# Gelu-and-multiply on one core: the second half of the first tile loaded through ScalarE's DMA queue instead of SyncE's

## The chip, the cores and the metric

The kernel runs on one core of one Trainium2 chip. The metric is the device time of one execution in microseconds (us); of several runs the median counts. Before the change three runs took 469.28, 469.09 and 472.29 us, median 469.28 us.

## What is computed

The input x has 32 x 512 rows of 2048 float32 numbers, 134.2 MB; the output has 1024 numbers for each row, 67.1 MB. The first half of each row goes through gelu and is multiplied by the second half:

```python
def reference(x: np.ndarray) -> np.ndarray:
    half_dim = x.shape[-1] // 2
    x1, x2 = (x[..., :half_dim].copy(), x[..., half_dim:].copy())
    gelu_x1 = 0.5 * x1 * (1 + erf(x1 / np.sqrt(2)))
    return (gelu_x1 * x2).astype(np.float32)
```

## The kernel before

The 16384 rows are cut into 16 tiles. A tile has 128 partitions with R = 8 consecutive rows in each, so a load of a whole tile brings 64 KB into each partition (8.39 MB), and a store of a whole tile takes 32 KB out of each (4.19 MB). There are two input buffers and two output buffers; tile i uses buffer i % 2 of each.

ScalarE computes the gelu from the input buffer into the output buffer (line 81), and VectorE multiplies the output buffer by the second half of the input in place (line 89). A middle tile is done in two pieces, of 5 and 3 rows; tile 0 and the last tile, 15, in three, of 2, 2 and 4 rows.

All waits are written by hand. Loads are issued by SyncE (`load`, line 46). Stores are issued by ScalarE's queue, in line with its gelus (`store`, line 51), except for those of tiles 14 and 15, which SyncE issues. A store first waits until VectorE has multiplied all that it takes out (semaphore mul_done). Tile 0 and tile 15 are stored in two halves of 4 rows; here they are called 0a, 0b, 15a and 15b.

Three loads stand ahead of the loop, in the program's first block (lines 60 to 64): the first half of tile 0 (rows 0 to 3 of each partition), its second half (rows 4 to 7), and all of tile 1. Each half of tile 0 has a semaphore of its own, first[0] and first[1]; ScalarE waits for it before the gelu of rows 0 to 1 and of rows 4 to 7 (lines 76 and 77). The block is closed at lines 66 and 67, where all engines meet. After that, load i + 2 is issued by SyncE as soon as tile i has been multiplied (lines 108 and 109). Load i + 2 and the store of tile i count on the same semaphore, ready[i % 2]; the first gelu of tile i + 2 waits for both (line 79), since it needs its input and overwrites the output buffer that the store reads.

ScalarE works in order. The store of 0a, with its wait for VectorE, stands on it ahead of the gelu of rows 4 to 7.

Of the kernel before, what the change touches and what calls it, by code (L numbers as in the profile page):

```python
# [1 line left out]

# [4 lines left out]

GELU = mybir.ActivationFunctionType.Gelu


@with_exitstack
def kernel(
    ctx: ExitStack,
    tc: tile.TileContext,
    x: bass.AP,
    out: bass.AP,
):
    nc = tc.nc
    P = nc.NUM_PARTITIONS

    x_flat = x.flatten_outer_dims()
    out_flat = out.flatten_outer_dims()
    n_rows, dim = x_flat.shape
    half = dim // 2

    R = 8
    x_t = x_flat.rearrange("(n p r) d -> n p r d", p=P, r=R)
    o_t = out_flat.rearrange("(n p r) d -> n p r d", p=P, r=R)
    n_tiles = x_t.shape[0]
    x_bufs = [nc.alloc_sbuf_tensor(f"x{k}_tile", [P, R, dim], x.dtype) for k in range(2)]  # L30
    o_bufs = [nc.alloc_sbuf_tensor(f"o{k}_tile", [P, R, half], out.dtype) for k in range(2)]

    first = [nc.alloc_semaphore(f"first{j}") for j in range(2)]
    ready = [nc.alloc_semaphore(f"ready{k}") for k in range(2)]
    gelu_done = nc.alloc_semaphore("gelu_done")
    mul_done = nc.alloc_semaphore("mul_done")
    tail_stored = nc.alloc_semaphore("tail_stored")
    n = {sem.name: 0 for sem in [*first, *ready, gelu_done, mul_done, tail_stored]}  # L40

    def counted(ins, sem, by):
        ins.then_inc(sem, by)
        n[sem.name] += by

    def load(i, rows, sem):
        ins = nc.sync.dma_start(out=x_bufs[i % 2][:, rows, :], in_=x_t[i][:, rows, :])  # L47
        counted(ins, sem, 16)
        return ins

    def store(queue, i, rows, sem):
        queue.wait_ge(mul_done, n[mul_done.name])
        counted(
            queue.dma_start(out=o_t[i][:, rows, :], in_=o_bufs[i % 2][:, rows, :]), sem, 16
        )

    for ins in (  # L60
        load(0, slice(0, 4), first[0]),
        load(0, slice(4, 8), first[1]),
        load(1, slice(0, 8), ready[1]),
    ):
        tc.no_tile_sem_insts.add(ins.ins.name)
    tc.close()
    tc.compile()  # L67

    for i in range(n_tiles):
        k = i % 2  # L70
        last = i == n_tiles - 1
        pieces = i == 0 or last
        steps = ((0, 2), (2, 4), (4, 8)) if pieces else ((0, 5), (5, 8))
        for lo, hi in steps:
            rows = slice(lo, hi)
            if i == 0 and lo % 4 == 0:
                nc.scalar.wait_ge(first[lo // 4], 16)
            elif lo == 0:
                nc.scalar.wait_ge(ready[k], n[ready[k].name])
            counted(  # L80
                nc.scalar.activation(  # L81
                    out=o_bufs[k][:, rows, :], in_=x_bufs[k][:, rows, :half], func=GELU
                ),
                gelu_done,
                1,
            )
            nc.vector.wait_ge(gelu_done, n[gelu_done.name])
            counted(
                nc.vector.tensor_mul(  # L89
                    out=o_bufs[k][:, rows, :],  # L90
                    in0=o_bufs[k][:, rows, :],
                    in1=x_bufs[k][:, rows, half:],
                ),
                mul_done,
                1,
            )
            if pieces and hi % 4 == 0:
                if last:
                    store(nc.sync, i, slice(hi - 4, hi), tail_stored)
                else:  # L100
                    store(nc.scalar, i, slice(hi - 4, hi), ready[k])
        if not pieces:
            if i == n_tiles - 2:
                store(nc.sync, i, slice(0, R), tail_stored)
            else:
                store(nc.scalar, i, slice(0, R), ready[k])
        if i + 2 < n_tiles:
            nc.sync.wait_ge(mul_done, n[mul_done.name])
            load(i + 2, slice(0, R), ready[k])


    nc.scalar.drain()  # L112
    for sem in (*first, *ready):
        nc.scalar.sem_clear(sem)
    nc.vector.drain()
    nc.vector.sem_clear(gelu_done)
    nc.sync.sem_clear(mul_done)
    nc.sync.wait_ge(tail_stored, n[tail_stored.name]).then_inc(
        tail_stored, -n[tail_stored.name]
    )  # L120


# [1 line left out]
_INS = ['x']  # L124
_OUTS = [((32, 512, 1024), 'float32')]


# [23 lines left out]
```

## Time and profile before

| What | Value |
|---|---|
| median of three runs | 469.28 us (469.09 to 472.29) |
| span of the profiled execution, first to last instruction | 467.9 us |
| median of the runs less that span | 1.4 us |
| DMA, whole span | 201.34 MB, 430 GB/s |
| VectorE busy | 140.5 us |
| ScalarE busy | 115.5 us |
| first half of tile 0: issue to landing | 12.0 us, from 0.73 |
| second half of tile 0: issue to landing | 21.3 us, from 1.16 |
| load 1: issue to landing | 45.5 us, from 1.64 |
| store 0a: issue to landing | 28.1 us, from 19.23 |
| store 0b: issue to landing | 41.0 us, from 30.57 |
| a middle load, a middle store: issue to landing | 44.2 us, 44.7 us |

The profile gives the span of the profiled execution and no other time of it; what lies around the span is read from the difference to the median. Times within the profile count from its first instruction. In the queue rows, q1 is the queue through which SyncE issues and q10 the one through which ScalarE issues; the columns are packets, MB, and the time that the packets took as a share of 16 DMA engines. In the row of tenths, each digit is one of 40 equal slices of the span. In a group's row there stand the count, the busy time, the mean duration in ns, and the idle time ahead of the group with what ended it. "SPq" and "ACTq" rows are issues of DMAs.

### The profile page before, as it was taken

The page shows a single profiled execution, that of the slowest core. Times are in us where ns is not written, and L with a number is a line of the kernel's source. Part 1 is how long each engine was busy: PE and PEld are TensorE (multiplying, and loading weights), DVE is VectorE, ACT ScalarE, POOL GpSimd, SP SyncE. Part 2 cuts the span into 40 slices and gives each one's busy share as a digit, 9 for nine tenths or more (in the row PEclk, how much of TensorE's full clock was granted, in tenths as well). Part 3 has the DMA queues.
Part 4 walks back from the last instruction along what each step waited for, and adds up shares of the span by engine and source line. Part 5 has one row for each costly group of instructions (what it writes and reads, how often), then busy time and mean ns, then how long its engine had stood idle before and what let it go on. Part 6 is the DMA issues. An engine that isn't in the chain of part 4 may idle for free.

```text
span 467.9 us, 152 instructions
## 1 busy us (share of the span) xinstructions
DVE 140.5 (30%) x34; ACT 115.5 (25%) x35; POOL 0.2 (0%) x4
## 2 busy tenths in 40 slices
DVE  0330514207052060511606116060150702507043
ACT  1320606042060410604106050050500506014060
POOL 0000000000000000000000000000000000000000
DMA  8999999999999999999999999999999999999998
GB/s 359 448 448 443 403 405 492 409 403 448 459 437 403 434 417 493 403 403 448 476 420 403 445 406 493 403 406 445 487 409 403 445 451 448 403 434 417 493 389 373
DMA packets 5041, 201.34 MB, mean 430 GB/s; under 512 B 560, under 2 KB 560, under 8 KB 560
## 3 DMA queue, kind: packets, MB, share of 16 engines
q1 hardware_dynamic: 2880, 142.61, 70.6%
q10 hardware_dynamic: 2160, 58.72, 29.1%
q14 instruction: 1, 0.01, 0.0%
HBM read 134.22 MB, written 67.11 MB: 430 GB/s over the span
## 4 chain that ended last, share of the span: by engine, by line
DMA 76%; DVE 14%; ACT 8%; ACTq 0%; SPq 0%; issue 0%
DMA out_dram<-o_tile 66%; DVE o_tile L89 14%; DMA x_tile<-in_x_dram 10%; ACT o_tile L81 8%; ACTq L112 0%; SPq L47 0%
## 5 line engine op out<-in xcount | busy, mean ns | idle before, releaser
L89 DVE TENSOR_TENSOR o_tile<-o_tile,x_tile 128x5120 f32<-128x5120 f32 (+3 forms) x34 | 140.5, 4171 | 319.7 <-ACT o_tile L81 319.7
L81 ACT ACTIVATE o_tile<-x_tile 128x5120 f32<-128x5120 f32 (+3 forms) x34 | 114.3, 3407 | 337.4 <-DMA out_dram<-o_tile 301.6
L81 ACT ACT_TABLE_LOAD x1 | 1.3, 1283 | 2.9 <-PEq L67 2.9
L135 POOL MEMSET const-bfloat16-1.0<- 128x1 bf16 x1 | 0.1, 101 | 0.0
L135 POOL MEMSET const-uint8-127<- 128x1 uint8 x1 | 0.1, 101 | 0.0
L135 POOL MEMSET const-float32-0.0<- 128x1 f32 x1 | 0.1, 98 | 0.2 <-issue 0.2
L135 POOL MEMSET const-float32-1.0<- 128x1 f32 x1 | 0.1, 98 | 0.0
## 6 DMA issues: line engine op xcount, KB each, us to landing
out_dram<-o_tile ACTq DMA_DIRECT2D x13, 4096.0 KB, 44.7
x_tile<-in_x_dram SPq DMA_DIRECT2D x2, 4096.0 KB, 16.6
out_dram<-o_tile ACTq DMA_DIRECT2D x2, 2048.0 KB, 34.5
out_dram<-o_tile SPq DMA_DIRECT2D x1, 4096.0 KB, 25.2
out_dram<-o_tile SPq DMA_DIRECT2D x2, 2048.0 KB, 7.8
x_tile<-in_x_dram SPq DMA_DIRECT2D x15, 44.2
```

The source lines that it names most:

```text
L81: nc.scalar.activation(out=o_bufs[k][:, rows, :], in_=x_bufs[k][:, rows, :half], func=GELU),
L89: nc.vector.tensor_mul(out=o_bufs[k][:, rows, :], in0=o_bufs[k][:, rows, :], in1=x_bufs[k][:, rows, half:],),
L135: nc = _bacc.Bacc("TRN2", target_bir_lowering=False, num_devices=1)
```

## The change

`load` gets a parameter for the engine that issues, with SyncE as its default, and the load of the second half of tile 0 is issued by ScalarE. Its place in the program, its semaphore and the data that it moves stay.

```diff
-    def load(i, rows, sem):
-        ins = nc.sync.dma_start(out=x_bufs[i % 2][:, rows, :], in_=x_t[i][:, rows, :])
+    def load(i, rows, sem, queue=nc.sync):
+        ins = queue.dma_start(out=x_bufs[i % 2][:, rows, :], in_=x_t[i][:, rows, :])
         counted(ins, sem, 16)
         return ins
...
     for ins in (
         load(0, slice(0, 4), first[0]),
-        load(0, slice(4, 8), first[1]),
+        load(0, slice(4, 8), first[1], nc.scalar),
         load(1, slice(0, 8), ready[1]),
     ):
```

## The prediction

> **What bounds the kernel now.** I read the page first, for the busy shares and the DMA row; then the chain of waits in order of time, for what releases each tile; then the DMA view of single stretches, for how the two queues share the engines; then the timeline of the first 48 us and of the end. The page:
>
> ```profile
> DVE 140.5 (30%) x34; ACT 115.5 (25%) x35; POOL 0.2 (0%) x4
> DMA  8999999999999999999999999999999999999998
> DMA packets 5041, 201.34 MB, mean 430 GB/s; under 512 B 560, under 2 KB 560, under 8 KB 560
> L81 ACT ACTIVATE o_tile<-x_tile 128x5120 f32<-128x5120 f32 (+3 forms) x34 | 114.3, 3407 | 337.4 <-DMA out_dram<-o_tile 301.6
> ```
>
> Both compute engines idle two thirds of the span; the DMA engines are at 90% or more in every slice but the first and the last. 201.34 MB at the 434 GB/s of the steady stretch below is 464 us of the 467.9 us span. So the time is DMA work plus whatever leaves the engines empty, and an edit that moves transfers without emptying them can only shift work about. The chain, two pieces of the loop and the end:
>
> ```profile
> 1.64 45.54 DMA x_tile<-in_x_dram
> 47.20 4.48 ACT o_tile L81
> 51.70 8.77 DVE o_tile L89 x2
> 60.50 40.04 DMA out_dram<-o_tile
> 100.56 4.48 ACT o_tile L81
> ...
> 403.86 44.69 DMA out_dram<-o_tile
> 448.56 1.91 ACT o_tile L81
> ```
>
> A tile waits for the store of the tile two before it. From landing to the next store is 13.3 us (4.48 + 8.77 and two gaps), the store lands 44.7 us after its issue, together 58 us for two tiles, or 29.0 us a tile: just what 12.58 MB take at 434 GB/s. How the queues share the engines (q1 is SyncE's, q10 ScalarE's), in 25 to 46 us and in 100 to 129 us:
>
> ```profile
> q1 hardware_dynamic: 110, 7.21, 79.5%
> q10 hardware_dynamic: 110, 1.80, 20.0%
> ```
> ```profile
> q1 hardware_dynamic: 144, 8.39, 66.7%
> q10 hardware_dynamic: 144, 4.19, 33.5%
> ```
>
> The two queues move equal numbers of packets whatever their size: one for one. Sizes and times follow. In the first stretch 7.21 MB / 110 is 64 KB and 1.80 MB / 110 is 16 KB. Every transfer is 128 data packets, 8 on each of the 16 engines; times on one engine, from the shares: whole load 2.42 us (66.7% x 29 x 16 / 128), whole store 1.21, half store 0.61. A half-tile load is 4 MB in 128 packets of 32 KB, so 1.21. A whole load beside a whole store takes 8 x 3.63 = 29.0 us, and they end together. That balance is the steady state.
>
> The start:
>
> ```profile
> 0.73 30.16 SPq L47 DMA_DIRECT2D x_tile<-in_x_dram  x4
> 12.76 3.71 ACT L81 ACTIVATE o_tile<-x_tile 128x2048 f32<-128x2048 f32 x2 [8.62 <-DMA x_tile<-in_x_dram]
> 14.70 4.49 DVE L89 TENSOR_TENSOR o_tile<-o_tile,x_tile 128x2048 f32<-128x2048 f32 x2 [14.70 <-ACT o_tile L81]
> 19.23 0.38 ACTq L54 DMA_DIRECT2D out_dram<-o_tile  x1
> 22.46 3.62 ACT L81 ACTIVATE o_tile<-x_tile 128x4096 f32<-128x4096 f32 x1 [5.99 <-DMA x_tile<-in_x_dram]
> 26.11 4.42 DVE L89 TENSOR_TENSOR o_tile<-o_tile,x_tile 128x4096 f32<-128x4096 f32 x1 [6.91 <-ACT o_tile L81]
> 30.57 0.36 ACTq L54 DMA_DIRECT2D out_dram<-o_tile  x1
> ```
>
> The halves land one after the other, at 12.7 and 22.4 us. First half landed to its store is 6.5 us; second half's gelu to its store 8.1 us.
>
> **The change, part by part.**
>
> *The issue.* SyncE loses one issue (0.42 us), so load 1 is issued 0.42 us sooner; ScalarE gains one of about 0.38 us, in the first block, where it otherwise waits for the block's end until its table load at 2.86 us. Behind it there stands only that table load (1.28 us), which must be done at 12.7 us. The first block ends when its last engine does, SyncE with three issues before, with two after. Cost 0; cover 8.6 us of ScalarE idle. On q1 load 1 now follows the first half directly; on q10 the new load is ahead of store 0a, which comes some 6 us after it is done.
>
> *The landing of the halves.* Two 32 KB streams one for one: 16 packets on each engine, 16 x 1.21 = 19.4 us, as before for both, but alternating. The second half still lands at 22.4. The first lands one packet sooner than the second or with it: 21.2 to 22.4 instead of 12.7. I take 21.2, since SyncE issues at 0.73 and ScalarE hardly before that.
>
> *Tile 0 on the compute engines.* Store 0a is issued 6.5 us after landing: 27.7 instead of 19.23 (+8.5). ScalarE runs in order, and the second half's gelu is queued behind that store's wait for mul_done: it starts at 28.1 instead of 22.46. Store 0b, and SyncE's load 2 that waits for the same multiply, go out at 36.2 instead of 30.57 (+5.6). Load 2 waits behind load 1 on q1 in any case until 43 us or later, so its late issue costs nothing.
>
> *What the DMA engines do meanwhile.* Nothing is idle: load 1 is on q1 from 22 us. With q10 empty it runs alone. By the trace's packet records store 0a, issued at 19.23, had its first packet at 24.38, behind packets that the engines had already taken up: 5 us. By that row it now starts near 33 to 34 us, and 4 or 5 of load 1's 8 packets have gone alone. Load 1's data end at 22.1 + 8 x 2.42 + 3 or 4 x 0.61 = 43.3 to 43.9, landing about 44.5 (before 47.18): tile 1 is 2.5 us early. Of the 16 half-store packets of tile 0, 12 or 13 are left, each behind a whole load packet: x 3.03 = 36 to 39 us, so store 0b lands at 81 to 83 instead of 71.5 (30.57 + 41.0). Tile 2 is 9 to 11 us late, and q1 is 4 or 5 packets ahead of where it stood against q10.
>
> *Where that lag goes.* Load 3 ends when its remaining 3 or 4 packets have alternated with store 1: 93.5 to 94.7. Load 4 is issued when tile 2 is multiplied: landing + 13.3 = 94.5 to 96.4, with about 1 us to its first packet when nothing is ahead (issue at 0.73, first packet at 1.74). So q1 runs dry for 1 to 5 us, q10 gets every turn, and store 1 catches up: its 8 packets are done at 99.5 (lead gone) to 104 (lead of 2 packets left), against 99.6 before. Generally a lead of k packets lasts only if (8 - k) x 3.63 exceeds the 14.9 us from store end to next load's first packet (0.5 from store 0b's last packet to its landing, + 13.3 + 1.0): k at most 3. I take 0 to 1, because the 5 us of the nearest row (store 0a) makes the dry spell long; ends 0 and 3.
>
> *The end.* Store 14 is issued on SyncE's queue behind load 15, 32 KB against 32 KB. With q1 ahead by k, load 15 ends k x 3.63 us before the point at which store 13 would otherwise finish, and store 13 shares with store 14: it lands 1.21 x k later than 448.54. The last store is issued at 460.26 + 1.21 k; it now stands 0.8 us in the queue behind store 15a (ready 1.0 after issue, first packet at 462.06). So the span grows by max(0, 1.21 k - 0.8): 0 at k = 0, 0.4 at 1, 1.6 at 2, 2.8 at 3. Below nothing: the first packet holds its engine 1.7 us (1.74 to 3.45) instead of 1.2, and two queues might cover that; no other emptiness is there to win, so -0.5 is the lower end.
>
> *Sum.* Issue 0, compute 0, DMA bytes 0, end +0.2 (between k = 0 and 1, less a little at the start). Span 467.9 + 0.2 = 468.1; the median of the three runs, 469.28, is 1.4 above the span, so 469.5 us.
>
> The Trainium skill, page "DMA: Bandwidth & Descriptors", section "Issuing engines are not separate DMA queues", says that transfers started from several engines interleave on the same 16 DMA engines, so that a second issuer saves only issue time. By it alone the sum would be 0.42 us less than before, 468.9; by the rows above it is 469.5, since the interleaving itself delays the first half by 8.5 us and has to be worked off.
>
> **The rivals.**
> *The lag is carried to the end* (slower). Tile 0's stores land 9 us late; were none of it worked off, store 13 would land 9 us late, tile 15's gelu with it, and the engines would empty after store 14 (458.1): +9.2 - 0.8 = +8.4, 477.7 us. It decides from a store 13 landing past 454, 5.5 us late. For it: a late store does delay its successor two tiles on. Against: with equal turns it needs a lead over 4 packets, and then q1 runs dry.
> *Part of it is carried*, k = 2 or 3: +1.6 to +2.8, 470.9 to 472.1.
> *Two loads together move slower than one.* For: no stretch of the trace has two load streams. Against: load beside store costs the plain sum, 2.42 + 1.21. If 10% of 19.4 us: +1.9, 471.2; 1% needs 24%.
> *The change doesn't do what it says*: the queues serve the first half first, because its descriptors stand earlier. Then all is as before, 469.3. Against: the one-for-one rows.
> *Faster*: the earlier tile 1 pulls the loop forward. Nothing to win, as the engines are full; -0.5 at best, 468.8; over 1% would need a higher DMA rate than any stretch shows.
>
> **How the numbers follow.** Forecast (lag worked off, k 0 to 1) 0.58; k = 2 or 3 0.16; no effect 0.08; small gain 0.03; slower mix 0.05, of which 0.02 beyond 1%; carried to the end 0.10, all beyond. About 1% (4.7 us) is what a measurement of this kernel can tell from no change; the three runs spread over 3.2. Faster by over 1%: 0.02, for a rate not seen. Slower by over 1%: 0.12. Within: 0.86. The range goes from the gain of 0.5 (468.8, rounded down to 468.7) to k = 3 (472.1, rounded up to 472.3), and leaves out what lies beyond.
>
> **What would show it.** Right: first gelu at 21 to 22.5 us, first store issue near 27.7 to 29, load 1 landed near 44.5, tile 2's first gelu at 81 to 83; then a stretch between 93 and 100 us in which q1 moves few packets; tile 3's gelu within 5 us of 100.6; tile 15's within 2.5 us of 448.56; DMA digits still 9 throughout. Wrong: a first gelu at 12.8 (no sharing); a tile 15 past 454 (lag carried); a DMA digit under 9 in the middle (an emptiness that I don't see); fewer GB/s in the first 22 us (slower mix).

## The result, and the profile after

The changed kernel takes 473.35 us, median of seven runs (471.01 to 473.85), against 469.27 us: ratio 1.007, 95% interval 1.0049 to 1.0091. It is 0.7% slower: inside the 1% that the prediction gave most of its chance, but 1.05 us above its range. Six of the seven runs of the kernel before lie between 469.09 and 469.28 us, the seventh took 472.29; the interval of the ratio leaves out 1. One run of all those below (485.12 us, of the kernel with the late gelu) was in a slower state and counts in no ratio. The profiled execution has a span of 472.4 us (before 467.9), 4.5 more.

The page of the changed kernel, the rows that answer to those shown of before:

```profile
DVE 140.5 (30%) x34; ACT 115.5 (24%) x35; POOL 0.2 (0%) x4
DMA  8998999999999999999999999999999999999978
DMA packets 5041, 201.34 MB, mean 426 GB/s; under 512 B 560, under 2 KB 560, under 8 KB 560
L81 ACT ACTIVATE o_tile<-x_tile 128x5120 f32<-128x5120 f32 (+3 forms) x34 | 114.3, 3407 | 343.4 <-DMA out_dram<-o_tile 309.0
```

The same packets and bytes, the same compute; ScalarE waits 7.4 us longer for stores. The last but one digit of the DMA row is a 7: the engines now idle near the end. Its start, from the timeline:

```profile
22.64 3.71 ACT L81 ACTIVATE o_tile<-x_tile 128x2048 f32<-128x2048 f32 x2 [18.98 <-DMA x_tile<-in_x_dram]
29.11 0.35 ACTq L54 DMA_DIRECT2D out_dram<-o_tile  x1
29.50 3.62 ACT L81 ACTIVATE o_tile<-x_tile 128x4096 f32<-128x4096 f32 x1 [3.16 <-DVE o_tile L89]
37.61 0.36 ACTq L54 DMA_DIRECT2D out_dram<-o_tile  x1
```

The halves share the DMA engines: the first gelu starts at 22.64 instead of 12.76, and the second half's gelu waits for VectorE behind store 0a. In 1.5 to 21.5 us each queue moved 128 packets:

```profile
q1 hardware_dynamic: 128, 4.19, 52.1%
q10 hardware_dynamic: 128, 4.19, 48.5%
```

From 22.3 to 34.1 us q1 then has the engines to itself (a packet counts in the stretch in which it begins, so that short stretches can show shares under or over 100%). The first row is the changed kernel's, the next ones are those of before in the same stretch:

```profile
q1 hardware_dynamic: 64, 4.19, 84.1%
```
```profile
q1 hardware_dynamic: 48, 3.15, 62.2%
q10 hardware_dynamic: 63, 1.03, 20.4%
```

With the packets that began just before, five of load 1's eight packets went on each engine ahead of store 0a's first, where before it was one: the loads are four packets ahead. Between 95.4 and 98.9 us, q1 is dry, that is, it has no load to move; its 9 packets are semaphore writes without data. The last row is that of q1 before, in the same stretch:

```profile
q10 hardware_dynamic: 41, 1.34, 88.8%
q1 hardware_dynamic: 9, 0.00, 0.1%
```
```profile
q1 hardware_dynamic: 16, 1.05, 69.1%
```

In that time three of q10's packets follow one another on each engine, where without a dry spell one comes between the end of a load and the next load: q10 takes back two of the four. Load 4 then begins; q1's packets from 98.8 to 99.5 us, and from 100.5 to 100.8 us:

```profile
q1 hardware_dynamic: 15, 0.98, 324.4%
```
```profile
q1 hardware_dynamic: 1, 0.07, 50.4%
```

Fifteen engines take up load 4 in the same turn; one takes another store packet first and begins load 4 one turn later.

The chain shows what came of it: tile 1 early, tile 3 late, and tile 15 later still.

```profile
1.16 44.22 DMA x_tile<-in_x_dram
45.41 4.48 ACT o_tile L81
58.70 46.98 DMA out_dram<-o_tile
105.69 4.48 ACT o_tile L81
...
350.98 45.37 DMA out_dram<-o_tile
396.37 4.48 ACT o_tile L81
409.66 44.41 DMA out_dram<-o_tile
454.10 1.91 ACT o_tile L81
```

Tile 15's gelu starts at 454.10 instead of 448.56, 5.54 us late; about 1.0 of that was slack at the end, which leaves the 4.5 us of the span. Stretches of the changed kernel, and after them the same two of before (the columns are the stretch and its length, VectorE, ScalarE and GpSimd busy, clock, DMA share, GB/s):

```profile
104.00:220.00 116.00, 35.04 (x8) 28.49 (x8) 0.00 (x0) 1.00 1.00 433
458.30:461.30 3.00, 2.23 (x2) 3.00 (x1) 0.00 (x0) 1.00 0.08 33
```
```profile
104.00:220.00 116.00, 35.04 (x8) 28.49 (x9) 0.00 (x0) 1.00 1.00 434
458.30:461.30 3.00, 1.94 (x1) 0.00 (x0) 0.00 (x0) 1.00 1.03 440
```

In the loop the engines are as full as before; at 458.3 to 461.3 us they stand at a share of 0.08 instead of 1.03: one engine of 16 is working, the others wait for store 15a.

The landing and packet records say which part is whose. A landing is 16 marks, one for each engine. For store 13, fifteen engines' marks lie between 450.93 and 451.29, the sixteenth's at 454.07 (before: all between 447.87 and 448.54).

Before, the last packet of a load is followed on every engine by the last one of the store beside it. Where k more packets of the store come behind that, the engine is said here to have a lead of k: its loads stand k packets ahead of the stores. There are two costs. Fifteen engines have a lead of two: store 13 is 2.75 us late on them (451.29 against 448.54), of which the prediction's formula gives 2.42 for k = 2. One engine took load 4 up one turn later, at 100.63 us instead of 98.9; it has a lead of one, and is said to be split off. Its mark comes 2.8 to 3.1 us after the rest. On it, 13 of the 64 KB packets after 100 us took longer than 2.42 us, by 3.70 us in all. Such packets, more than 0.08 us over 2.42, are called long below; the kernel before has none after 100 us.

### The profile page after: what moved, and what is told of

It is laid out like the page before. It is cut to its first block, busy times and chain, and to the rows that moved or that the text cites. A ratio compares the mean times of both kernels' runs of the same rounds, so it can differ in the third digit from the quotient of the medians.

```text
span 472.4 us, 152 instructions
## 1 busy us (share of the span) xinstructions
DVE 140.5 (30%) x34; ACT 115.5 (24%) x35; POOL 0.2 (0%) x4
## 4 chain that ended last, share of the span: by engine, by line
DMA 76%; DVE 14%; ACT 8%; ACTq 0%; issue 0%; SPq 0%
DMA out_dram<-o_tile 67%; DVE o_tile L89 14%; DMA x_tile<-in_x_dram 9%; ACT o_tile L81 8%; ACTq L112 0%; SPq L47 0%
```

## The experiments

Theory: order. The late first half lets the loads get ahead of the stores; the lead, and engines split in their order, make tile 15 late. Rivals: two load streams at once, or the issue from ScalarE, cost the time; or the late engine alone does. A dry spell is a time in which q1 has nothing to move, a refill is the first load after it. Beside each result stands the time of the kernel before on the same chip; diffs are against the kernel named.

**Late gelu without two queues** (against the kernel before).

```diff
                 nc.scalar.wait_ge(first[lo // 4], 16)
+                if lo == 0:
+                    nc.scalar.wait_ge(first[1], 16)
```

> Both halves of tile 0 are loaded by SyncE, one after the other, as before; only the gelu of rows 0 to 1 also waits for the second half, so that it starts at 22.4 us as in the changed kernel. Order theory (tile 0's stores come late, the loads get ahead, SyncE's queue runs dry near 95 to 99 us, one engine or more comes back out of step): the changed kernel's time without its two queues, 471 to 474 us, store 0b landed near 81 us, tile 15's gelu at 452 to 455 us. Rival (two load streams at once, or the issue from ScalarE, cost the time): 469.3 us and tile 15's gelu at 448.6 us.

Measured: 470.61 us against 469.21, ratio 1.0033 (1.0019 to 1.0047). Runs went from 469.68 to 472.41, and one to 485.12. A cost appears without two queues, but only a third of it; the time lies between the two expectations (471 to 474, and 469.3). The activation table's load fell behind the added wait, so the first gelu started at 23.86 us, 1.2 later than in the changed kernel. In the profiled execution (471.9 us) the lead fell to 0 on all engines; thirteen engines end store 13 by 449.03 us, two by 449.63, and one at 451.31. That one has three long packets, 2.0 us over in all, the first of them at the refill. So the first lag doesn't carry over as such: how it is worked off decides.

**Two queues without a late first half** (against the changed kernel).

```diff
-        load(0, slice(0, 4), first[0]),
-        load(0, slice(4, 8), first[1], nc.scalar),
+        load(0, slice(0, 2), first[0]),
+        load(0, slice(2, 4), first[0], nc.scalar),
+        load(0, slice(4, 6), first[1]),
+        load(0, slice(6, 8), first[1], nc.scalar),
...
-                nc.scalar.wait_ge(first[lo // 4], 16)
+                nc.scalar.wait_ge(first[lo // 4], 32)
```

> Tile 0 is loaded in four quarters, SyncE and ScalarE taking one quarter of each half, so that two load streams run at once from the start as in the changed kernel, but the first half still lands first. Order theory: first gelu at 12.8 us, second half at 22.5 us, stores as before, tile 15's gelu within 1 us of 448.6, time 469.0 to 470.0 us. Rival (sharing of the engines by two load queues costs, or puts an engine out of step): 471 to 474 us although the first gelu is at 12.8 us.

Measured: 469.22 us against 469.21, ratio 1.000 (0.999 to 1.0009). Its chain ends as that of before:

```profile
403.76 44.71 DMA out_dram<-o_tile
448.49 1.91 ACT o_tile L83
```

The first gelu is at 12.97 us. Load streams on both queues cost nothing as long as the first half lands first.

**Store 14 behind store 13, in both kernels.** The same edit in the changed kernel and in the one before.

```diff
-                store(nc.sync, i, slice(0, R), tail_stored)
+                store(nc.scalar, i, slice(0, R), tail_stored)
```

> The changed kernel, with the store of tile 14 issued by ScalarE behind store 13 instead of by SyncE behind load 15, so that store 13 shares the engines with nothing once load 15 is done. Lead theory (15 engines stand two packets ahead on SyncE's queue, and store 13 pays 1.21 us for each packet when it alternates with store 14): store 13 lands some 1.2 to 2.4 us sooner than 454.1, span 1 to 2.4 us shorter, 471 to 472.5 us; what is left over 469.3 belongs to the engine out of step. Rival (the lead has no share in it, all is the one late engine): the span stays within 0.5 us of the changed kernel's, 473 to 474 us.

> The kernel before with the same move of store 14, as a control. Lead theory: in the kernel before there is no lead, load 15 and store 13 end together, so nothing changes: 469.3 us within 0.5. Rival (where store 14 stands matters by itself, whatever the lead): 1 us or more faster or slower.

Measured: changed kernel 473.27 us, before 469.28, against 469.21. The control shows no change. In the changed kernel the median moved by 0.1 us, as the rival said, though thirteen of store 13's marks came down from 451 to between 448.40 and 448.91, as the lead theory said. Three engines were split off in its profile, with marks at 450.34, 451.86 and 452.47, and the last one, which went from store 14 straight into 15a and 15b, set the time. Where an engine is split off, the lead of the others is hidden behind it.

**A smaller lag, without two queues** (against the kernel before); the second kernel has the move of store 14 as well.

```diff
-        load(0, slice(0, 4), first[0]),
-        load(0, slice(4, 8), first[1]),
+        load(0, slice(0, 6), first[0]),
+        load(0, slice(6, 8), first[1]),
```

> The kernel before, with its first two loads cut at 6 and 2 rows instead of 4 and 4, both on SyncE's queue: the first lands near 17.6 us instead of 12.7, so tile 0's first store is 4.9 us late, half of the changed kernel's 9.9. Out-of-step theory (what costs is that SyncE's queue runs dry and some engine comes back out of step; a lead of 2 or 3 packets alone lasts without a dry spell and costs 1.21 us a packet at store 13, less 0.8): all 16 engines in step, store 13 landed at 451 to 452, span 469.5 to 470.8, 470.9 to 472.2 us, runs within 0.5 of one another. Rival (any late first store puts an engine out of step, which then loses time in every tile): runs spread over 1 us or more, one engine last. Second rival (a lag this small is worked off): 469.3 us.

> The same cut at 6 and 2 rows, with store 14 issued by ScalarE behind store 13, so that store 13 doesn't alternate with it. Lead theory: the lead then costs nothing at the end, store 13 lands at 448.5 and the time is the kernel before's, 469.0 to 469.7 us, 1.6 to 2.8 less than with the same cut alone. Rival (an engine out of step): as with the cut alone, within 0.3 us of it, as in the changed kernel, where the move won 0.1 us.

Measured: 471.07 us against 469.27, ratio 1.0039 (1.0024 to 1.0054), four runs within 0.32; with store 14 moved 469.73, ratio 1.001 (1.0001 to 1.002). Last marks of store 13: 451.24 and 449.08. No packet is long in either. This is the lead of two packets by itself, all engines in step, and what it costs: 1.8 us, most of it given back when store 13 alternates with nothing.

**Load 1 in small packets** (against the changed kernel).

```diff
-        load(1, slice(0, 8), ready[1]),
+        *(load(1, slice(r, r + 2), ready[1]) for r in range(0, 8, 2)),
```

> The changed kernel, with load 1 issued in four pieces of 2 rows, so that its packets are 16 KB and alternate one for one with tile 0's half stores. Order theory: tile 0's stores catch up during load 1 (12 of their 16 packets are out when it ends, instead of 3 or 4), store 0b lands near 61 us instead of 81.6, SyncE's queue never runs dry near 95 us, no engine gets out of step, tile 15's gelu within 1 us of 448.6: 469.0 to 470.0 us, though the halves still share the engines and the first gelu stays at 22.6 us. Rival (the late first gelu or the shared halves cost by themselves): 472 to 474 us.

Measured: 469.86 us against 469.27, ratio 1.0012 (1.0003 to 1.0022). Its first store is issued as late as the changed kernel's, and nearly all of the cost is gone:

```profile
22.74 3.71 ACT L81 ACTIVATE o_tile<-x_tile 128x2048 f32<-128x2048 f32 x2 [17.53 <-DMA x_tile<-in_x_dram]
29.21 0.35 ACTq L54 DMA_DIRECT2D out_dram<-o_tile  x1
```
```profile
405.50 43.28 DMA out_dram<-o_tile
448.80 1.91 ACT o_tile L81
```

The late half itself costs 0.6 us at most. The rest is what the packet sizes of the next load make of it: here the loads end one packet behind the stores (store 13's last mark is at 446.39, load 15's at 448.78, and the chain's row is named for the store though it ends with the load), and no packet is long.

**The queues exchanged** (against the changed kernel).

```diff
-        load(0, slice(0, 4), first[0]),
-        load(0, slice(4, 8), first[1], nc.scalar),
+        load(0, slice(0, 4), first[0], nc.scalar),
+        load(0, slice(4, 8), first[1]),
```

> The changed kernel with the roles exchanged: ScalarE loads the first half, SyncE the second half and tile 1. Order theory: which queue has which half doesn't matter, both land at 22 to 23 us, 471 to 474 us with one or a few engines out of step. Rival (the place of the second half on ScalarE's queue, ahead of its stores, is what costs): 469.3 to 470 us.

Measured: 471.59 us against 469.27, ratio 1.0063 (1.0041 to 1.0086), runs from 471.14 to 473.47. The profiled execution, one of 471.14, has all 16 engines in step at a lead of two (marks of store 13 from 450.91 to 451.48) and no long packet after 100 us. That is the floor; it agrees with the 471.07 of the cut at 6 and 2.

**One engine made late by itself** (against the kernel before).

```diff
+    def extra():
+        ins = nc.scalar.dma_start(out=o_bufs[1][0:17, 0, 0:512], in_=x_t[0][0:17, 0, 0:512])
+        counted(ins, ready[1], 16)
+        return ins
...
     for ins in (
+        extra(),
```

> The kernel before, both halves on SyncE's queue, with one more transfer in the first block: ScalarE loads 17 partitions of 2 KB into a part of the second output buffer that tile 1's gelu overwrites. It is meant to run on a single DMA engine, which falls some 1.5 us behind the other 15 in the first 22 us and stays there. Out-of-step theory (an engine that stands apart from the others loses 0.1 to 0.6 us in single packets tile after tile): its last load and store packets take visibly longer than 2.42 and 1.21 us in many tiles, the spread of the 16 landings grows towards the end, and the time is 471.5 us or more, runs spread by 1 us. Rival (an engine that is late stays just as late and costs no more than its own delay, less 0.8 us of slack at the end): 469.5 to 470.8 us, the spread of landings the same in all tiles.

Measured: 471.98 us against 469.25, ratio 1.0059 (1.0044 to 1.0074), runs within 0.74. Two engines stand apart in the profile. The one with the extra transfer has a lead of 0 and is late: from 102.8 to 450.8 us its stores end exactly 29.00 us apart, tile after tile, so it loses nothing in the loop. Its delay was not the 1.5 us expected but 2.6 at 102.8 us, and its mark of store 13, 451.32, is the last: 2.8 us later than before. That is the cost, and it is the rival's reason, though the time is in the theory's range. A second engine missed a turn when store 0a began (its first packet at 27.55 us, the others' by 26.05) and has a lead of one. It has the three long packets after 100 us, 0.31 us in all; its stores end 29.09 us apart on average, up to 422.8 us, and the spread of a store's ends over the engines grows from 3.1 us to 3.7 (at 420 us), as the theory said. So an engine that is merely late loses nothing more; one with a lead of one does, here 0.09 us a tile.

**The changed kernel again.**

> The changed kernel once more, unaltered, for a second profile and more runs beside the same kernel before. Theory (a lead of 2 packets on all engines gives a floor near 471.1 us; engines that come back out of step after the dry spell add up to 3 us, differently in each execution): runs from 471.0 to 474, and the profile's span above 469.7 us equals what its last engine lost in long packets. Rival (one fixed cost): runs within 0.5 us of one another.

Measured: 473.38 us against 469.25, runs from 472.17 to 473.51. This time fourteen engines had a lead of two (marks of store 13 from 450.77 to 451.33) and two were split off, with a lead of one (451.80 and 453.60). All 20 long packets are on these two, 2.03 us and 3.55 us. The span, 471.9, is 2.2 above 469.7, and not 3.55 as the theory had it; but an engine with a lead of one saves 1.21 us at the end by the prediction's formula, and 3.55 less 1.21 is 2.3. By the same working the first profile's engine gives 2.5, where its span is 2.7 above.

**Load 4 shifted against the turn** (the first two against the changed kernel, the third against before).

```diff
-        steps = ((0, 2), (2, 4), (4, 8)) if pieces else ((0, 5), (5, 8))
+        steps = ((0, 2), (2, 4), (4, 8)) if pieces else ((0, 4), (4, 8))
```

The second kernel has ((0, 6), (6, 8)) there.

> The changed kernel with the middle tiles done in pieces of 4 and 4 rows instead of 5 and 3: landing to store takes 12.5 us instead of 13.3, so load 4 is issued 0.8 us sooner, at 94.1. Edge theory (in the changed kernel load 4 arrives just as a queue's turn is given, and one engine misses it): with 0.8 us to spare all 16 engines take load 4 up in the same turn, at 97.7 or 98.9, none out of step; a lead of 2 gives 471.1, of 3 gives 472.2 us, runs within 0.5 of one another, landings of a store within 0.6 us in every tile. Rival (engines split at any refill after a dry spell): 472 to 474 us, runs spread over 1 us, landings of a store 2 to 5 us apart.

> The changed kernel with the middle tiles in pieces of 6 and 2 rows: landing to store 14.2 us, load 4 issued 0.9 us later, at 95.8. Edge theory: all engines miss the turn at 98.9 and take load 4 up at 100.1, the lead falls to 1, the end costs about 0.4 us: 469.5 to 470.3 us, runs within 0.5 us. If the arrival falls on the next edge, some engines split off again and runs spread by 1 to 3 us. Rival (engines split at any refill after a dry spell): 471.5 us or more, one engine last.

> Control: the kernel before with the middle tiles in pieces of 4 and 4 rows. Both theories: the DMA engines are full, so 0.8 us less from landing to store changes nothing, 469.3 us within 0.4.

Measured against 469.27: 472.17 us for 4 and 4, 477.14 for 6 and 2 (473.79 to 477.99), 469.77 for the control (two of its ten runs near 472), which itself cost 0.5 and so a little more than expected. With 4 and 4 one engine was split off all the same; but fifteen stood at a lead of three, the split one at two, there was no long packet, and 472.17 is the price of a lead of three. With 6 and 2 fifteen engines stood at a lead of one and one at two; the time, expected 0.4 us up, rose by 7.9. The profile, of the slowest run (477.99), has 299 long packets, 88.8 us over 16 engines. The edge theory fell; the lead of one came in view.

**The lead by itself, one and three packets** (against the kernel before).

```diff
-        load(0, slice(0, 4), first[0]),
-        load(0, slice(4, 8), first[1]),
+        load(0, slice(0, 5), first[0]),
+        load(0, slice(5, 8), first[1]),
```

The second kernel cuts at 7.

> The kernel before, with its first two loads, both on SyncE's queue, cut at 5 and 3 rows: the first lands near 15.1 us, tile 0's first store is 2.4 us late, one more packet of load 1 goes ahead of it, so that all engines stand one packet ahead. Lead-of-one theory (an engine whose load is one packet ahead of the stores has a packet 0.1 to 0.7 us too long in every tile): long packets on most engines near one per 29 us, the steady loop over 29.0 us a tile, 472 us or more. Rival (a lead alone costs 1.21 us a packet at the end, less 0.8; the long packets need an engine that differs from the others, or a dry spell): 469.5 to 470.0 us, no long packets after 60 us.

> The same with a cut at 7 and 1 rows: the first load lands near 20.1 us, the first store is 7.3 us late. Lead theory: a lead of 3 packets on all engines, no dry spell (or one at its very edge), no long packets in the loop, store 13 landed 1.21 x 3 = 3.6 us late, time 471.8 to 472.4 us. Rival (a lag of this size makes SyncE's queue run dry and splits the engines): runs spread over 1 us or more, 471 to 474 us.

Measured against 469.20: cut at 5 477.73 us, ratio 1.0181 (1.0166 to 1.0196); cut at 7 472.75, ratio 1.0075 (1.0058 to 1.0092). With the cut at 7, all engines have a lead of three: fifteen have store 13's marks near 452.1, 3.6 us late as expected, and one at 453.4, which puts the time 0.35 us over the expected range. With the cut at 5, where all loads are on one queue and in the order of before, all engines have a lead of one, and the loop itself is slower. Stretches of it, and after that the same of the cut at 6:

```profile
104.00:220.00 116.00, 35.04 (x8) 27.81 (x8) 0.00 (x0) 1.00 1.00 428
220.00:336.00 116.00, 35.04 (x8) 28.49 (x8) 0.00 (x0) 1.00 1.00 425
336.00:444.00 108.00, 35.04 (x8) 28.49 (x8) 0.00 (x0) 1.00 1.00 425
```
```profile
104.00:220.00 116.00, 35.04 (x8) 28.49 (x8) 0.00 (x0) 1.00 1.00 434
220.00:336.00 116.00, 35.04 (x8) 28.49 (x8) 0.00 (x0) 1.00 1.00 434
```

Full engines in both (share 1.00), 2% fewer bytes in one. Its chain:

```profile
103.32 4.48 ACT o_tile L81
...
457.62 1.91 ACT o_tile L81
```

Tiles 3 to 15 take 354.3 us, 29.5 a tile, where before takes 348.0 (100.56 to 448.56), 29.0 a tile. Of its 64 KB packets between 100 and 450 us, 291 are longer than 2.42 us by more than 0.08, 95.2 us over 16 engines or 6.0 on each: 0.5 in each of the 12 tiles. That is most of the 8.5 us by which the run is slower.

## Why the prediction was wrong

Right: the issue costs nothing. The halves share one for one and land together (22.6 and 22.8 us; I had 21.2 for the first). Store 0a at 29.1, at the upper end of 27.7 to 29; load 1 landed at 45.4, 1.8 us early, where I had 44.5; store 0b at 81.6 (81 to 83); then the dry spell on q1, near 95 to 99. Load 1 was issued at 1.16 us instead of 1.64, so the issue time was saved and won nothing. The rival of a lag carried to the end in full, 477.7, did not come. Its sign did, barely: store 13 landed at 454.07, past 454. But only one engine was that late, and for a reason that the rival didn't have; the other fifteen were done by 451.29. Tile 3's gelu, at 105.69, was just outside the 5 us that I had allowed.

The sum had +0.2 us for the end and nothing for the rest; measured are 4.1 us.

Wrong, first, in "where that lag goes": "I take 0 to 1". On fifteen engines the lead that stayed was 2, a case that I had priced at 1.6 us and given 0.16 together with 3; the cut at 6 and 2 measures it at 1.8. The loads were four packets ahead, as I had it (4 or 5), and lost only two of them in the dry spell. Load 4 was issued at 94.9, and its first packets came at 98.9, 4.0 us later: less than the 5 us I went by, though that row was the right kind. (In the bound on k, 0.5, 13.3 and 1.0 make 14.8 and not 14.9; it stays at 3.)

Wrong, second and larger, in the same step: the sixteen engines were treated as one. At the refill one engine missed the turn, and came back with a lead of 1. No term of the sum and none of the rivals had an engine of its own.

Wrong, third, in "the end": 0.4 us for a lead of one, by a formula in which the loop itself costs nothing. With a lead of one on all engines the loop loses 0.5 us a tile, and the run takes 8.5 us more (cut at 5 and 3). In the changed kernel it falls on one or two engines, costs one of them up to 3.7 us, and tile 15 waits for the last. These two make the difference between the 471.1 floor and the 473.28 and 473.75 of the two profiled executions. Two profiles of the changed kernel had one and two engines split off, and one of the exchanged queues, at 471.14 us, none; that the whole spread from 471.0 to 473.9 comes of this is likely, but the other executions were not profiled.

The rule of the Trainium skill that was weighed ("DMA: Bandwidth & Descriptors", "Issuing engines are not separate DMA queues") holds in what it says: the engines are shared, and only issue time is saved (load 1 issued 0.48 us sooner). The 0.42 us that it would have credited does not show in the time (469.22 us with both queues from the start, 469.21 without).

Left open: why a load that is one packet ahead of the stores has long packets, and one that is 0, 2 or 3 ahead hardly any. With the cut at 5 the long packet is mostly the second or third one of a load, once or twice in a tile on each engine; what holds it up, no record shows. Nor does one show why one engine misses a turn that fifteen get.

## What to carry to other kernels

When transfers fill the engines for the whole run, ask of a change to one queue not only what it moves, but in which order the queues stand against each other afterwards: that order lasted here from the first 100 us to the end at 470. Two transfers that are needed one after the other are best not issued side by side on two queues, since each then lands when both do (22.6 and 22.8 us here, instead of 12.7 and 22.4); where both queues are to be used, split each of them over both, as the quarters did at no cost. A semaphore that counts 16 engines waits for the last one, so a landing's sixteen marks are worth reading before its median.

## What the runs showed of the hardware

A steady loop of 64 KB load packets alternating with 32 KB store packets ran at 434 GB/s with the load 0, 2 or 3 packets ahead and at 425 to 428 with the load one ahead, at the same DMA share of 1.00: the lost time is counted as busy, inside packets of 2.5 to 3.3 us instead of 2.42. A queue that begins while the other is busy waits: issue to first packet 4.0 us (load 4, 94.9 to 98.9) and 5.1 us (store 0a, 29.1 to 34.2), against 1.0 us with nothing ahead (the first load, 0.73 to 1.74). An engine that missed a turn at a refill kept its other place to the end: its load 4 began at 100.63 us, the others' at 98.9, and its store 13 ended at 454.07 us, the others' by 451.29.
